# The small stack fourth instead of first, and a ring of expert slabs that starts with six buffers

## The chip, the cores and the metric

The kernel runs on one core of a Trainium2 chip. The metric is the device time of one execution in microseconds (us). Before the change the median of three runs is 1639.17 us (1639.06 to 1639.73).

## What is computed

One decoder layer for 256 tokens of width 2048, all in 32-bit floats. The first part mixes tokens by two paths (latent attention and a gated linear recurrence). The change touches the second part only, the mixture of experts:

```python
g_sel = jnp.argmax(g_logits, axis=-1)                   # one of 4 groups of experts
top_p, top_i = lax.top_k(jax.nn.softmax(e_in, axis=-1), TOP_K)   # two of its 8 experts
weights = g_w[:, None] * top_p / jnp.sum(top_p, axis=-1, keepdims=True)
...
hg = jnp.einsum('td,edf->tef', t, w_gate_e[sl])         # 2048 x 512 for each expert
hu = jnp.einsum('td,edf->tef', t, w_up_e[sl])
act = jax.nn.silu(hg) * hu * comb[:, sl, None]
out = out + jnp.einsum('tef,efd->td', act, w_down_e[sl])   # 512 x 2048
```

Of 32 experts each token uses two, so most experts see few tokens, but the weights of nearly all of them must be read: 12 MiB for each.

## The kernel before

The mixer and the router take the first 780 us or so. The router counts the tokens of each expert and sorts the experts by that count: rank 0 is the expert with the most tokens. Expert number 0 and the expert of rank 0 are computed *dense*, for all 256 tokens; ranks 1 and 2 form a *stack* in which each expert has 64 columns of TensorE for its tokens, and ranks 3 to 26 form six stacks of four experts with 32 columns each. A last stack (ranks 27 to 30) and a loop for experts with too many tokens run only if there is something to do.

Each expert's weights lie in DRAM as 12 slabs of 1 MiB, 8 for gate and up and 4 for down. A stack goes through them in 12 *groups*: a group takes the same slab of each of its experts, so two or four slabs, and multiplies them side by side on TensorE (line 1285). Group 0 to 7 are gate and up (`gu`), then follows the activation (`s`, the transposes `ab`, the copy `aT`), and groups 8 to 11 are down (`yb`), each followed by multiplies that put the tokens back (`ob`). Before a stack begins, its tokens are gathered (`prep`, the tiles `cb`, `xb`, `xg`). A group is 8 multiplies of 64 columns with two experts, and 16 of 32 columns with four.

The slabs of the stacks land in a *ring* of buffers (`fetch_used`). As long as the list `room` has an entry, a load takes a new buffer; then each load takes the oldest buffer of the ring and has to wait until TensorE is through with the group that reads it. Loads are issued by SyncE's queue in the order in which the code calls for them, and one that waits holds up all behind it. I number them: load 1 is the first into the ring, and there are 312.

Dense experts use other buffers. Their slabs (`raw` for the first six, then `rawb`, two buffers) are split by ScalarE and VectorE into a high and a low half (`whl`, lines 186 and 187), and 48 multiplies (lines 199 to 201) use each slab. The ring's buffers come from the pool `big` of nine, in which `raw` lives too, so a ring buffer can have to wait for a dense slab to be split.

The main loop interleaves two streams: `heavy` (the dense experts) and `light` (the stacks), by the share of each that is done. A light step is one group and counts its slabs, 2 or 4; a dense step counts 0.5. After a stack's activation one dense step is put in between. When the dense stream has ended, which it does after 120 loads, five more buffers join the ring, one with each group (`later`). The order on SyncE is the order of the code; on the other engines a scheduler places the instructions at build time.

Of the kernel before, what the change touches and what calls it, by code (L numbers as in the profile page):

```python
# [29 lines left out]
B2 = 10  # L30
SKIP = [0, 1]
BIG2 = 4
RING = 7
EARLY = (1, 1)
AHEAD2 = 6
AHEAD_B = 2
# [29 lines left out]

DENSE = 0
HEAVY = [("dense", 0)]
LIGHT = [("stack", 1, 2)] + [("stack", r, 4) for r in (3, 7, 11, 15, 19, 23)]
LAST = ("stack", 27, 4)  # L70


# [1 line left out]
def decoder_layer_kernel(ctx, tc, xT, c, pos, cols_d, const_d, mask_d, w_ada, w_head, w_half, w_blk, w_mlv, w_pa, w_pb, w_out,  # L74
# [988 lines left out]

    ring = []

    room = [u8] * RING

    def fetch_used(src, rank):
        if room:
# [145 lines left out]
    def expert(r):  # L1215
        if r not in reg:
            reg[r] = nc.sync.value_load(R["order"][0:1, r:r + 1], min_val=0, max_val=NE - 1)
        return reg[r]
# [143 lines left out]
    def unit(u):  # L1362
        if u[0] == "dense":
            r = u[1]
            return dense(lambda: expert(r), lambda: R["perm"][:, r:r + 1].to_broadcast([32, P]), lambda: R["qT"][:, 1], xgh, xgl)
        return stack(u[1], u[2], u is LIGHT[-1])

    def stream(units, gen=None):
        ready = lambda u: u[0] == "dense" or u[1] in pre
        for i in range(-1 if gen else 0, len(units)):  # L1370
            if i >= 0:
                if not ready(units[i]):
                    pre[units[i][1]] = prep(*units[i][1:])
                gen = unit(units[i])
            for what in gen:
                if what != "act":
                    yield what
                else:
                    if i + 1 < len(units) and not ready(units[i + 1]):
                        pre[units[i + 1][1]] = prep(*units[i + 1][1:])  # L1380
                    yield "act"

    heavy, light = stream(HEAVY, first), stream(LIGHT)
    n_light = 12.0 * sum(u[2] for u in LIGHT)
    n_heavy = HEAVY_SHARE * n_light
    streams, total, done = [heavy, light], (n_heavy, n_light), [started, 0.0]
    forced, later = [], [v8] * 2 + [w8] * W4
    while any(streams):
        i = forced.pop(0) if forced else int(done[0] / total[0] > done[1] / total[1])
        if not streams[i]:  # L1390
            i = 1 - i
        got = next(streams[i], None)
        if got == "act":
            forced = [1 - i] * SKIP[i]
        elif got:
            done[i] += got
            if not streams[0] and later:
                room.append(later.pop(0))
        else:
            streams[i] = None  # L1400
# [158 lines left out]
```

## Time and profile before

| what | value |
|---|---|
| median of three runs | 1639.17 us |
| profiled execution | 1639.2 us, of which the traced span is 1637.3 us |
| TensorE (PE) busy | 1378.5 us, 84% of the span |
| VectorE (DVE) busy | 815.3 us, 50% |
| ScalarE (ACT) busy | 504.2 us, 31% |
| moved by DMA | 560.96 MB, mean 343 GB/s |
| chain that ended last | 33% of it in loads into the ring |

The busy shares are means over two unlike halves. Up to about 780 us TensorE is busy nearly without a break; in the stacks it is not, and the transfers are. Which of the two a stretch waits for is read from the views by stretch.

### The profile page before, as it was taken

What the parts mean: (1) busy time and instruction counts of PE and PEld (TensorE: products, weight loads), DVE (VectorE), ACT (ScalarE), POOL (GpSimd) and SP (SyncE); (2) the same over time, 40 slices, a digit from 0 to 9 for tenths busy, and PEclk for the clock granted to TensorE, in tenths of its full rate; (3) what the DMA queues carried; (4) which work ended last, traced back from release to release, by engine and by line L of the source; (5) the groups of instructions that cost most, each with busy time, mean ns of one, the idle gap of its engine ahead of it and who ended that gap; (6) DMA issues with size and microseconds to landing.
All of it is one profiled execution on the core that took longest, in us unless ns stands there. A gap on an engine that the chain in (4) does not pass through costs nothing.

```text
span 1637.3 us, 24656 instructions
## 1 busy us (share of the span) xinstructions
PE 1378.5 (84%) x9726; PEld 1009.6 (62%) x9726; DVE 815.3 (50%) x1177; ACT 504.2 (31%) x720; POOL 87.4 (5%) x91
## 2 busy tenths in 40 slices
PE   7899998999999999999989689868767656657675
PEld 5698997999999989999747356535413213213212
DVE  5878699879776789986414233224301201201102
ACT  3134765446755574445312121212001001001000
POOL 0150014000000010121000000000000000000000
PEclk9899999999999999999999889998868878888888
DMA  9978767878676779874597999999999999999995
GB/s 383 374 283 329 282 212 283 327 286 296 245 273 242 269 267 416 321 297 155 224 409 273 416 400 378 420 417 393 399 421 422 420 422 421 420 422 421 421 421 228
DMA packets 78462, 560.96 MB, mean 343 GB/s; under 512 B 8705, under 2 KB 8961, under 8 KB 11905
## 3 DMA queue, kind: packets, MB, share of 16 engines
q1 hardware_dynamic: 78050, 558.84, 86.5%
q8 instruction: 80, 1.31, 0.3%
q10 hardware_dynamic: 288, 0.45, 0.1%
q14 instruction: 44, 0.36, 0.1%
HBM read 569.74 MB, written 2.10 MB: 349 GB/s over the span
## 4 chain that ended last, share of the span: by engine, by line
PE 50%; DMA 33%; DVE 6%; ACT 3%; issue 2%; POOL 1%; SPq 0%; DVEq 0%; POOLq 0%; ACTq 0%
DMA ring<-in_w_gu_dram 22%; DMA ring<-in_w_dn_dram 11%; PE gu L1285 6%; PE ga L199 4%; PE yb L1285 4%; PE ga L201 3%; PE ga L200 3%; DVE whl L187 2%; PE hp L201 2%; PE hp L199 2%; PE hp L200 2%; PE xb L1259 2%; PE wo L199 1%; DVE raw L143 1%; PE wo L201 1%
## 5 line engine op out<-in xcount | busy, mean ns | idle before, releaser
L1285 PE MATMUL gu<-ring,xg 128*32 128x512 f32 (+1 forms) x1664 | 270.4, 756 | 138.0 <-DMA ring<-in_w_gu_dram 138.0
L187 DVE TENSOR_TENSOR whl<-raw,whl 128x1024 fp32r<-128x1024 f32 (+1 forms) x222 | 267.1, 1210 | 93.1 <-ACT whl L186 92.6
L186 ACT ACTIVATE whl<-raw 128x1024 fp32r<-128x1024 f32 (+1 forms) x222 | 229.5, 1038 | 255.3 <-PE ga L201 62.7
L1285 PEld LDWEIGHTS gu<-ring,xg 128*32 128x32 f32 (+1 forms) x1664 | 65.7, 136 | 324.6 <-DMA ring<-in_w_gu_dram 172.0
L143 DVE SCALAR_TENSOR_TENSOR raw<-raw,cond 128x2048 f32<-128x2048 f32 x96 | 220.3, 2296 | 16.5 <-DMA raw<-in_w_ada_dram 16.4
L1285 PE MATMUL yb<-ring,aT 128*32 128x512 f32 (+1 forms) x832 | 130.7, 725 | 64.0 <-DMA ring<-in_w_dn_dram 61.9
L199 PE MATMUL ga<-hh,whl 128*128 128x256 f32 x512 | 149.6, 292 | 0.0
L201 PE MATMUL ga<-hh,whl 128*128 128x256 f32 x512 | 145.0, 283 | 1.4 <-DVE whl L187 1.3
L200 PE MATMUL ga<-hl,whl 128*128 128x256 f32 x512 | 144.8, 283 | 0.0
L1285 PEld LDWEIGHTS yb<-ring,aT 128*32 128x32 f32 (+1 forms) x832 | 33.5, 131 | 145.2 <-issue 99.6
L1231 DVE SCALAR_TENSOR_TENSOR xs<-ob,mod,xs 128x256 f32<-128x256 f32 x112 | 46.5, 477 | 131.9 <-PE ob L1325 131.9
L1251 DVE TENSOR_REDUCE wc<-cb 128x1 f32<-128x256 f32 x7 | 3.0, 424 | 215.8 <-PE cb L1248 215.8
L199 PEld LDWEIGHTS ga<-hh,whl 128*128 128x128 f32 x512 | 97.9, 191 | 5.1 <-issue 3.5
L201 PEld LDWEIGHTS ga<-hh,whl 128*128 128x128 f32 x512 | 97.9, 191 | 2.0 <-DVE whl L187 2.0
L200 PEld LDWEIGHTS ga<-hl,whl 128*128 128x128 f32 x512 | 98.0, 191 | 1.0 <-issue 0.7
L187 DVE TENSOR_TENSOR whl<-rawb,whl 128x1024 fp32r<-128x1024 f32 x36 | 43.0, 1221 | 110.7 <-ACT whl L186 110.7
L1303 ACT ACTIVATE s<-gu 128x512 f32<-128x512 f32 x7 | 4.2, 594 | 295.8 <-PE gu L1285 295.8
L201 PE MATMUL hp<-hh,whl 128*128 128x256 f32 x320 | 91.7, 287 | 3.4 <-DVE whl L187 3.3
L199 PE MATMUL hp<-hh,whl 128*128 128x256 f32 x320 | 92.6, 290 | 0.0
L200 PE MATMUL hp<-hl,whl 128*128 128x256 f32 x320 | 91.2, 285 | 0.0
L1314 ACT ACTIVATE yh<-yb 128x512 fp32r<-128x512 f32 x28 | 16.8, 599 | 190.2 <-PE yb L1285 190.2
L186 ACT ACTIVATE whl<-rawb 128x1024 fp32r<-128x1024 f32 x36 | 36.7, 1050 | 122.6 <-DMA rawb<-in_w_gu_dram 59.7
(418 smaller groups left out, 2905.6 us busy)
## 6 DMA issues: line engine op xcount, KB each, us to landing
ring<-in_w_gu_dram SPq DMA_DIRECT2D x208, 1024.0 KB, 14.8
ring<-in_w_dn_dram SPq DMA_DIRECT2D x104, 1024.0 KB, 15.1
raw<-in_w_ada_dram SPq DMA_DIRECT2D x96, 1024.0 KB, 6.8
raw<-in_w_blk_dram SPq DMA_DIRECT2D x32, 1024.0 KB, 5.1
raw<-in_w_half_dram SPq DMA_DIRECT2D x20, 1024.0 KB, 6.9
raw<-in_w_out_dram SPq DMA_DIRECT2D x16, 1024.0 KB, 6.5
raw<-in_w_head_dram SPq DMA_DIRECT2D x16, 704.0 KB, 7.8
rawb<-in_w_gu_dram SPq DMA_DIRECT2D x10, 1024.0 KB, 10.4
```

Source lines behind the costliest of these rows:

```text
L143: vec.scalar_tensor_tensor(raw, raw, 1.0, cond, op0=ALU.mult, op1=ALU.mult, accum_out=mod[:, i:i + 1])
L186: keep(act.activation(hi, raw, AF.Copy))
L187: keep(vec.tensor_tensor(lo, raw, hi.bitcast(F32), op=ALU.subtract))
L199: pe.matmul(out, wh, xh, start=first, stop=False)
L200: pe.matmul(out, wh, xl, start=False, stop=False)
L201: pe.matmul(out, wl, xh, start=False, stop=last)
L1231: vec.scalar_tensor_tensor(xs[:, d], src, mod[:, 80 + d:81 + d], xs[:, d], op0=ALU.mult, op1=ALU.add)
L1251: vec.tensor_reduce(wc, cb[:, :T], axis=AX.X, op=ALU.add)
L1259: pe.matmul(b[:, i * P:(i + 1) * P], xr[tt][:, k * P:(k + 1) * P], gt[tt], start=tt == 0, stop=tt == 1)
L1285: return lambda: pe.matmul(out[j * C:(j + 1) * C, :], x[:, k * P + j * C:k * P + (j + 1) * C], ws[j][:, cut], start=first, stop=stop)
L1303: act.activation(s, gu[0], AF.Silu)
L1314: act.activation(yh, yb, AF.Copy)
```

## The change

The list of stacks has the stack of ranks 1 and 2 in fourth place instead of first; ranks 3, 7 and 11 come ahead of it. The ring starts with six buffers instead of seven, and a seventh is added to `room` once 12 slabs are done, so that load 13, the first of the fourth group, takes it. The five later buffers join as before.

```diff
-RING = 7
+FIRST_RING = 6
...
-LIGHT = [("stack", 1, 2)] + [("stack", r, 4) for r in (3, 7, 11, 15, 19, 23)]
+LIGHT = [("stack", r, 4) for r in (3, 7, 11)] + [("stack", 1, 2)] + [("stack", r, 4) for r in (15, 19, 23)]
...
-    room = [u8] * RING
+    room = [u8] * FIRST_RING
...
             done[i] += got
+            if i == 1 and done[1] == 4 * FIRST_RING / 2:
+                room.append(u8)
             if not streams[0] and later:
                 room.append(later.pop(0))
```

On SyncE's queue, loads 6 to 8 of the ring stood like this before. The names `DVE`, `PE`, `Activation` and `DMAHW` in brackets are the semaphores that an instruction waits for: the engine that has to be through, or an earlier transfer. A `TENSOR_LOAD` reads whether an expert has tokens.

```order
L1071 DMA ring<-in_w_gu_dram 128x2048 [waits DMAHW6_49,DVE_49]
L1071 ISA
L1071 DMA ring<-in_w_gu_dram 128x2048 [waits DMAHW7_49,DVE_49]
L1224 TENSOR_LOAD order
L1224 ISA x2
L1074 ISA
L1074 REGISTER_ALU
L1074 ISA
L1074 DMA ring<-in_w_gu_dram 128x2048 [waits DMAHW1_49,DMAHW0_49,PE_49]
```

And now, loads 6 and 7:

```order
L1071 DMA ring<-in_w_gu_dram 128x2048 [waits DMAHW6_49,DVE_49]
L1224 TENSOR_LOAD order
L1224 ISA x2
L1074 ISA
L1074 REGISTER_ALU
L1074 ISA
L1074 DMA ring<-in_w_gu_dram 128x2048 [waits DMAHW7_49,DMAHW1_49,PE_49]
```

The seventh load waited for a dense slab (VectorE); it now waits for TensorE to be through with the first group. The new seventh buffer stands six loads further on, as load 13, ahead of load 14:

```order
L1074 DMA ring<-in_w_gu_dram 128x2048 [waits DMAHW6_49,PE_49]
L1071 ISA
L1071 DMA ring<-in_w_gu_dram 128x2048 [waits DVE_49]
L1074 ISA
L1074 REGISTER_ALU
L1074 ISA
L1074 DMA ring<-in_w_gu_dram 128x2048 [waits DMAHW7_49,PE_49]
```

On TensorE the first stack's last gate and up groups, the gather for the second stack (`cb`, `xb`) and the first down groups stood like this before, where `64x512 x40` are five groups of two slabs:

```order
L201 MATMUL gu<-xgh,whl 128x258
L1285 MATMUL gu<-ring,xg 64x512 x40
L1248 MATMUL cb<-const,G 128x128 x2
L1259 MATMUL xb<-G,xr 128x128 x8
L1285 MATMUL gu<-ring,xg 64x512 x8
L1259 MATMUL xb<-G,xr 128x128 x24
L1308 MATMUL ab<-const,s 128x128 x4
L1285 MATMUL yb<-ring,aT 64x512 x16
```

And now, where `32x512 x48` are three groups of four slabs:

```order
L201 MATMUL gu<-xgh,whl 128x258
L1285 MATMUL gu<-ring,xg 32x512 x48
L1248 MATMUL cb<-const,G 128x128 x2
L1259 MATMUL xb<-G,xr 128x128 x24
L1285 MATMUL gu<-ring,xg 32x512 x16
L1259 MATMUL xb<-G,xr 128x128 x8
L1308 MATMUL ab<-const,s 128x128 x4
L1285 MATMUL yb<-ring,aT 32x512 x32
```

Between these groups stand the first dense expert's multiplies, 261 of its gate and up part from the first gather on. Before, in the order of the program: 31, group 0 of the stack of two, 23, group 1, 15, groups 2 to 6, the last gate and up group, three down groups with 25 dense multiplies between, 23, then 63, group 0 of the stack at rank 3, 74, its group 1, and the last 7. Now: 69, groups 0 and 1 of the stack at rank 3, 68, group 2, 74, group 3, 50, and groups 4 to 6 behind one another.

## Rows read from the trace of the kernel before

**Rows 1.** The page's section 2: 40 equal slices of the span

```profile
DMA  9978767878676779874597999999999999999995
GB/s 383 374 283 329 282 212 283 327 286 296 245 273 242 269 267 416 321 297 155 224 409 273 416 400 378 420 417 393 399 421 422 420 422 421 420 422 421 421 421 228
```

**Rows 2.** Busy time by stretch: length, engines (instructions), TensorE clock, DMA share, GB/s

```profile
800.00:811.00 11.00, 11.00 (x68) 6.45 (x68) 2.45 (x2) 2.12 (x2) 0.00 (x0) 1.00 0.03 7
811.00:850.00 39.00, 34.27 (x187) 16.81 (x183) 6.71 (x17) 7.38 (x16) 0.00 (x0) 0.96 1.01 412
850.00:875.00 25.00, 25.00 (x151) 14.88 (x152) 11.43 (x25) 6.38 (x11) 0.00 (x0) 1.00 0.97 361
875.00:900.00 25.00, 24.88 (x206) 18.80 (x204) 7.45 (x11) 3.95 (x8) 0.00 (x0) 1.00 0.55 218
900.00:960.00 60.00, 40.43 (x304) 22.25 (x304) 17.83 (x34) 8.18 (x10) 0.00 (x0) 0.87 1.01 413
960.00:1000.00 40.00, 36.40 (x289) 25.64 (x289) 15.51 (x27) 11.35 (x17) 0.00 (x0) 0.89 0.91 361
1100.00:1150.00 50.00, 40.85 (x317) 27.58 (x318) 24.00 (x49) 12.84 (x20) 0.00 (x0) 0.90 0.94 381
```

**Rows 3.** What SyncE's transfer queue waited for, 780 to 900: total, times, longest

```profile
SPq L1074 <- PE gu L1285: 33.7, 6, 14.6
SPq L1071 <- DVE whl L187: 22.8, 2, 16.0
SPq L1074 <- PE yb L1285: 15.4, 3, 8.9
```

**Rows 4.** Timeline of SyncE: issues into the ring (start, us to the last's end)

```profile
809.62 0.33 SPq L1071 DMA_DIRECT2D ring<-in_w_gu_dram  x1
885.58 2.62 SPq L1074 DMA_DIRECT2D ring<-in_w_gu_dram  x4
```

**Rows 5.** The ring's instructions, 780 to 830: from issue to landing

```profile
DMA to landing us min/median/max: 4.7/10.5/13.8
```

**Rows 6.** Timeline of TensorE: first dense multiply, first group, the group of load 8

```profile
797.75 0.36 PE L199 MATMUL gu<-xgh,whl 128*128 128x258 f32 x1
801.64 0.65 PE L1285 MATMUL gu<-ring,xg 128*64 128x512 f32 x2
817.91 3.65 PE L1285 MATMUL gu<-ring,xg 128*64 128x512 f32 x16 [0.50 <-DMA ring<-in_w_gu_dram]
```

**Rows 7.** The chain that ended last: start, us, what (x counts trace records)

```profile
791.08 6.92 PE xb L1259 x62
801.71 3.58 PE gu L1285 x16
881.99 3.57 PE gu L1285 x32
908.46 6.07 DMA ring<-in_w_gu_dram
914.57 5.19 PE gu L1285 x32
919.76 7.19 DMA ring<-in_w_gu_dram
927.00 3.66 PE gu L1285 x32
```

**Rows 8.** Busy time by stretch, as in rows 2: one wait, and the later stacks

```profile
1140.00:1145.00 5.00, 3.86 (x20) 0.99 (x24) 0.00 (x0) 0.00 (x0) 0.00 (x0) 0.50 1.01 424
1200.00:1600.00 400.00, 259.24 (x1674) 88.61 (x1666) 44.87 (x106) 22.61 (x44) 0.00 (x0) 0.82 1.01 421
```

## The prediction

> **What bounds the kernel now.** I read four views in this order. First the page's row of bytes per second: from about the 23rd of its 40 slices on it stands near 420 GB/s until the last slice [rows 1]. The second half of the program is a stream of expert weights, and its length is the bytes left divided by that rate, plus every microsecond in which the transfers did not run at it. So I looked for those microseconds, with the busy times by stretch [rows 2]. 1 MiB at 421 GB/s takes 2.49 us. Measured against 421, the stretches lose (length times one minus rate over 421): 800 to 811, 10.8 us; 811 to 850, 0.8; 850 to 875, 3.6; 875 to 900, 12.1; 900 to 960, 1.1; 960 to 1000, 5.7; 1100 to 1150, 4.8; after 1200 nothing. About 39 us in all, and each one that goes away ends the program one microsecond sooner, as long as nothing later runs dry instead.
>
> Who made the queue wait there is told by the waits of the transfer queue between 780 and 900 [rows 3]: for a ring buffer that TensorE still reads (33.7 and 15.4 us), and for the seventh buffer, which held a dense slab until VectorE had split it (22.8 us). The issue times show both: the seventh load goes out at 809.62 although the first six had landed by 800, and nothing goes out until 885.58 after the loads had run out at about 877 [rows 4]. Between 875 and 900 TensorE is busy 24.88 of 25 us [rows 2]: this is the passage from the stack of two to the first stack of four. There the scheduler put 63 and then 74 dense multiplies around the first group of four, while the ring held seven loads, one group and three quarters. No buffer came free, so no load could go out.
>
> **The change, step by step.** The bytes stay the same: the same 26 ranks, the same 12 slabs each, the same dense slabs at the same numbers of loads. So the sum is made of idle stretches of the transfer queue alone. The bricks, each from a row: a load lands at the earliest 4.7 us after its issue [rows 5], which is 2.2 us and then 2.49 us of bytes; loads behind it follow every 2.49 us. TensorE starts a group 1.1 us after its last load landed (load 7 goes out at 809.62, so load 8 lands at 816.8, and the group starts at 817.91 [rows 4, 6]). A group takes 3.6 us, of two slabs or of four alike, and 5.3 us when TensorE had waited some microseconds before it [rows 7]. A dense multiply takes 0.12 us: 31 of them fill 797.75 to 801.64 [rows 6]. A gather multiply takes 0.22 us: 62 records, two to a multiply, fill 6.92 us [rows 7].
>
> I call groups 0 to 7 the gate and up groups of the stack at rank 3, which now comes first. Before group 0 stand 69 dense multiplies instead of 31: 797.75 + 69 x 0.12 = 806.0, and group 0 ends at 809.6. Loads 7 to 10 take its buffers and run from 811.8. Before, load 7 also ran from 811.8, so the first gap stays as it is: the seventh buffer no longer blocks the queue, but group 0 is later by as much. This edit I cost at nothing.
>
> Then come new gaps, since a group now takes four of six buffers. Group 1 needs load 8 (816.8), starts at 817.9 after 8.3 us of waiting, ends at 823.2. Loads 7 to 10 ran out at 821.8, and loads 11 to 15 run from 825.4: a gap of 3.6. (Load 13 is the seventh buffer; its dense slab is split by then, as the dense multiplies that use it stand before group 0. Were it not, loads 14 and 15 would wait behind it.) 68 dense multiplies last until 831.4; group 2 runs 831.5 to 835.1, in time: no gap. 74 more, and group 3 runs 844.0 to 847.6, while the queue is full only until 847.8: gap 2.0. 50 more; group 4 runs 853.6 to 857.2, no gap. Group 5 starts when load 24 has landed, 863.4, ends at 868.7: gap 1.2. Group 6 likewise, 874.5 to 879.8: gap 1.1. 26 gather multiplies and transposes, then group 7, 885.6 to 889.2: no gap. Group 8, the first down group, 895.6 to 900.9: gap 1.1. Together 9.0 us, and load 40 has landed at 811.8 + 34 x 2.49 + 9.0 = 905.5.
>
> Before, load 40 stood behind the losses of 811 to 900, 0.8 + 3.6 + 12.1, and about 0.8 of those up to 912: 17.3 us. The stream is then ahead by 17.3 - 9.0 = 8.3 us. The 12.1 us go because the passage from a stack of two to a stack of four no longer happens beside the dense expert: the order has the first dense expert's 261 remaining gate and up multiplies done before group 4, where before the last of them stood behind the second group of four. The 3.6 us of 850 to 875 are a lower rate at a busy share of 0.97 [rows 2], while few loads were under way; I let them go too, since groups of four put four loads in the queue at a time, and from 900 to 960, where they did so, the rate was 413 [rows 2].
>
> After load 40 the dense slabs stand at the same loads in the queue, and the ring grows by five at the same load, so the rest moves as a block. Two things in it are unlike. The passages inside and between stacks beside the dense experts cost 5.7 us at 960 to 1000 and 4.8 at 1100 to 1150 [rows 2]. After the change, the passage inside the stack at rank 7 is in the order what the costly one of before was (24 dense, 32 gather, 24 dense multiplies on end between groups), and the passage inside the stack at rank 3 now stands before the dense down work and is in the gap of 1.1 already. What remains is whether the second is gone or moves to the stack at rank 11: between 0 and 4.8 us of gain. I take 0, the rate rows of the stack having no other cause that goes. The stack of two itself now runs on twelve buffers: 5.0 us of loads to a group of 3.6 us. Its group can be later than the loads by ten buffers, 24.9 us, before the queue notices; I cost it at nothing.
>
> TensorE's waits have a price of their own. A group after 6.07 us of waiting took 5.19 us, one after 7.19 us, with dense work in the middle of it, 3.66 [rows 7]; that is in the sum as 5.3 for groups 1, 5, 6 and 8. The Trainium skill has a rule for this (TensorE: Matmul & The Clock Gate, section "Loop structure matters more than you think"): a wait for a transfer in the middle of a loop lets the clock fall to half. It speaks against a ring of six, which adds such waits, and the trace agrees. Without its effect, with 3.6 us for every group, the gaps would shrink to about 3.9 us and the sum would be -13.4, some 1626.
>
> The sum is made against the profiled execution, 1639.2 us for a span of 1637.3; the median of the runs is 1639.17, the same within 0.1. 1639.2 - 8.3 = 1630.9, say 1631.
>
> **The rivals.** *The starved ring* (slower). While only a few loads are under way, the rate may be the 361 GB/s of 850 to 875 [rows 2] instead of 421. If all of loads 7 to 40 run so, 34 x 2.49 x (421/361 - 1) = 14.1 us come on top: -8.3 + 14.1 = +5.8, 1645. It decides from a mean rate, while busy, of about 380 on. Against it: at 811 to 850 as few loads were under way, and the rate was 412 [rows 2].
> *The late stack of two* (slower). Where TensorE idles, the granted clock is 0.50, and 0.82 on average after 1200 [rows 8]. At half clock a group takes 7.2 us and needs loads of 5.0; eight groups fall 17.6 us behind, the gather of the next stack takes 13.8, four down groups 8.8 more: 40 us against a cover of 24.9. The queue stops for 15, and the end is 1639.2 - 8.3 + 15 = 1646. It decides when the lag passes 24.9 us. Against it: the same groups ran at 0.96 and 1.00 from 811 to 875 [rows 2], where TensorE had work without end.
> *The round trip is longer than I count.* If the answer from a group's end to a landed load is 1.3 us longer in each of the five gaps, 6.5 of the 8.3 us are eaten: 1637, no change that can be told. For it: the middle time to landing is 10.5 us [rows 5], though mostly by queueing.
> *More is gained.* The passage at 1100 to 1150 goes too: 1639.2 - 8.3 - 4.8 = 1626.
>
> **Chances.** Forecast 0.54, more gained 0.20, longer round trip 0.13, starved ring 0.09, late stack of two 0.04. A measurement can tell about 0.2%, 3.3 us, from no change. Faster: the forecast (but for 0.02 at its upper edge) and the larger gain, 0.72; same: the round trip and that edge, 0.15; slower: 0.13. The range reaches from the larger gain with 2 us to spare, 1624, to just past the round trip's case, 1640; beyond it lie the two slower rivals.
>
> **What will show it.** Right: between 800 and 811 the queue idle as before; four short gaps and no long one up to 905; TensorE waiting some 8 us before the second group of the stream, then 5 to 6 us before groups 5 and 6; no stretch without a load at 877 to 887; the ring's fifth load of growth about 8 us earlier than before; 421 GB/s on twelve buffers throughout the stack of two. Wrong: a rate below 400 with a busy share near 1 before 905 (starved ring), a queue that waits for a TensorE group of the stack of two (late stack), or the lead of 8 us that is there at load 40 and gone at load 125.

## The result, and the profile after

Eight runs of the changed kernel have a median of 1631.42 us, eight of the kernel before 1640.26; the ratio is 0.9947, with a 95% interval of 0.993 to 0.9963. That is 8.7 us less by the ratio (6 to 11.5 by its interval), where 8.3 were forecast. The size of the whole was right, in part by luck: the lead that was forecast for load 40 came out too large, and what was forecast to stay the same behind it did not.

Busy time by stretch in the kernel after; the columns are those of [rows 2], the last one is GB/s:

```profile
811.00:850.00 39.00, 34.51 (x275) 24.90 (x276) 7.33 (x11) 5.30 (x5) 0.00 (x0) 0.89 0.88 354
850.00:875.00 25.00, 13.87 (x92) 4.51 (x94) 0.00 (x0) 0.69 (x4) 0.00 (x0) 0.77 0.93 380
875.00:900.00 25.00, 20.27 (x158) 10.81 (x150) 4.79 (x11) 4.74 (x10) 0.00 (x0) 0.88 0.97 398
900.00:960.00 60.00, 44.39 (x312) 28.24 (x309) 26.62 (x51) 10.28 (x13) 0.00 (x0) 0.83 0.94 368
960.00:1000.00 40.00, 33.08 (x260) 21.31 (x264) 9.66 (x12) 6.01 (x6) 0.00 (x0) 0.96 1.01 421
1100.00:1150.00 50.00, 37.17 (x274) 23.07 (x270) 16.47 (x28) 7.59 (x9) 0.00 (x0) 0.90 0.96 392
1200.00:1600.00 400.00, 272.54 (x1707) 98.30 (x1711) 55.17 (x132) 25.01 (x48) 0.00 (x0) 0.86 1.01 421
```

The long hole is gone: 218 GB/s from 875 to 900 in [rows 2], now 398. In its place the queue is a little short of bytes from 811 to 875, and again from 900 to 960. Loss against 421 GB/s in us, worked out as in the prediction (length times one minus rate over 421) from one row for each stretch, for the two traces of before and three of after:

| stretch | before | before again | after | after again | after, third |
|---|---|---|---|---|---|
| 797 to 811 | 11.5 | 11.7 | 11.4 | 11.9 | 11.6 |
| 811 to 850 | 0.8 | 0.7 | 6.2 | 6.6 | 6.3 |
| 850 to 900 | 15.6 | 15.4 | 3.8 | 3.8 | 3.8 |
| 900 to 960 | 1.1 | 1.3 | 7.6 | 4.7 | 4.6 |
| 960 to 1000 | 5.7 | 5.8 | 0.0 | 0.0 | 0.0 |
| 1000 to 1100 | 0.5 | 2.1 | 4.5 | 3.3 | 3.6 |
| 1100 to 1200 | 5.0 | 5.7 | 3.6 | 2.9 | 3.8 |
| sum in us | 40.2 | 42.7 | 37.1 | 33.2 | 33.7 |

The chain that ended last shows what the gaps are made of (start, us, what). It goes from the first group to the down groups of the first stack:

```profile
803.18 3.70 PE gu L1285 x32
808.13 7.22 DMA ring<-in_w_gu_dram
815.49 5.54 PE gu L1285 x32
829.38 3.57 PE gu L1285 x32
842.01 3.57 PE gu L1285 x32
851.80 3.59 PE gu L1285 x32
855.39 6.25 DMA ring<-in_w_gu_dram
861.67 6.36 PE gu L1285 x32
868.03 4.76 DMA ring<-in_w_gu_dram
872.83 5.87 PE gu L1285 x32
...
884.44 3.59 PE gu L1285 x32
888.02 6.99 DMA ring<-in_w_dn_dram
895.15 4.98 PE yb L1285 x32
900.13 7.03 DMA ring<-in_w_dn_dram
907.30 5.71 PE yb L1285 x32
```

Each long group stands behind a wait for a load, each short one behind dense or gather work, as [rows 7] had it. Read these times from the first load into the ring, not from the start: that load was issued at 779.66 here and at 782.77 in the first trace of before, and in the repeats at 782.05, 781.08 and 781.70, so a lead of 3 us is not in every trace of the change, and it arises ahead of the first load into the ring.

### The profile page after: what moved, and what is told of

It reads as the page before. It is cut to its first block, busy times and chain, and to the rows that moved or that the text cites. A ratio compares the mean times of both kernels' runs of the same rounds, so it can differ in the third digit from the quotient of the medians.

```text
span 1632.3 us, 24652 instructions
## 1 busy us (share of the span) xinstructions
PE 1360.1 (83%) x9726; PEld 1004.2 (62%) x9726; DVE 816.4 (50%) x1177; ACT 504.9 (31%) x720; POOL 90.5 (6%) x91
## 4 chain that ended last, share of the span: by engine, by line
PE 51%; DMA 34%; DVE 9%; ACT 3%; issue 2%; POOL 0%; SPq 0%; DVEq 0%; POOLq 0%; ACTq 0%
DMA ring<-in_w_gu_dram 22%; DMA ring<-in_w_dn_dram 11%; PE gu L1285 6%; PE ga L199 4%; PE ga L201 4%; PE ga L200 4%; DVE raw L143 4%; PE yb L1285 3%; DVE whl L187 2%; PE hp L201 2%; PE hp L199 2%; PE hp L200 2%; PE xb L1259 2%; PE wo L199 1%; PE wo L201 1%
## 5 line engine op out<-in xcount | busy, mean ns | idle before, releaser
L1285 PE MATMUL gu<-ring,xg 128*32 128x512 f32 (+1 forms) x1664 | 256.5, 714 | 131.2 <-DMA ring<-in_w_gu_dram 131.0
L1285 PEld LDWEIGHTS yb<-ring,aT 128*32 128x32 f32 (+1 forms) x832 | 33.7, 131 | 156.9 <-issue 115.9
L201 PE MATMUL gu<-xgh,whl 128*128 128x258 f32 x256 | 72.1, 285 | 2.2 <-DVE whl L187 2.2
```

The lines of the kernel that those rows point to most:

```text
L201: pe.matmul(out, wl, xh, start=False, stop=last)
L1285: return lambda: pe.matmul(out[j * C:(j + 1) * C, :], x[:, k * P + j * C:k * P + (j + 1) * C], ws[j][:, cut], start=first, stop=stop)
```

## The experiments

**Which half of the change does it.** The new list with the old ring, and the new ring with the old list.

```diff
-LIGHT = [("stack", 1, 2)] + [("stack", r, 4) for r in (3, 7, 11, 15, 19, 23)]
+LIGHT = [("stack", r, 4) for r in (3, 7, 11)] + [("stack", 1, 2)] + [("stack", r, 4) for r in (15, 19, 23)]
```

> The new list of stacks, with the old ring of seven from the start. Theory A (the gain is the passage from a stack of two to a stack of four that no longer stands beside the dense expert): all of the gain stays, and as much as 3 us more, since load 7 then needs only a split dense slab and may go out before the first group ends: 1626 to 1632 where the kernel before takes 1640, ratio 0.991 to 0.996. Theory B (the gain is the seventh buffer that no longer blocks the queue): no gain is left, 1638 to 1642, ratio 0.999 to 1.001.

Measured: 1625.95 us, ratio 0.9926 (0.9904 to 0.9947). The other half alone, the six buffers and the seventh from 12 slabs on:

> The old list of stacks, with the ring of six and the seventh buffer joining once 12 slabs are done. Theory A: the 10 us without a transfer at the passage from two to four stay; only load 7 goes out some 4 us sooner, at the end of the first group of two: 1636 to 1640, ratio 0.997 to 1.000. Theory B: the gain of the change is here, 1630 to 1633, ratio 0.993 to 0.996.

Measured: 1635.84 us, ratio 0.9977 (0.9963 to 0.999). Both as theory A had them by the ratio; both medians lie at the lower edge of its range, 0.05 and 0.2 us below. The list alone takes 14 us by the medians and 12 by the ratio, more than the whole change; the ring alone takes 4 with the old list. These 4 us rest on the twelve runs: the kept trace of the second kernel is of its slowest run, 1645.0 us. The hole at the passage is still there in the second kernel, by its stretch:

```profile
875.00:900.00 25.00, 24.09 (x199) 18.02 (x197) 7.37 (x11) 4.25 (x8) 0.00 (x0) 1.00 0.53 214
```

The two halves don't add up: 12 and 4 apart, 9 together, all by the ratios. With the old list the ring of six frees the queue of a load that waits for a dense slab: load 7 goes out 22.6 us after the first load, where it was 26.9. With the new list that slab is split sooner, since 69 dense multiplies stand ahead of the first group; load 7 goes out before the first group, not after it. Issue of load 7, in the new list with the old ring, and in the second trace of the changed kernel:

```profile
804.72 0.33 SPq L1071 DMA_DIRECT2D ring<-in_w_gu_dram  x1
```

```profile
809.16 0.33 SPq L1074 DMA_DIRECT2D ring<-in_w_gu_dram  x1
```

Counted from the first load (781.62 and 782.05) that is 23.1 against 27.1 us. The two kernels had not run side by side so far; now they did:

> The new list with the old ring of seven once more, beside the changed kernel on the same chip. Theory A (the ring of six costs what load 7 waits longer, the end of the first group instead of a split slab, some 3 us): 1624 to 1629, 2 to 6 us below the changed kernel. Rival I (the two rings are alike, and the difference between the two kernels was chance): within 1.5 us of it.

> The changed kernel once more, for the pair with the old ring in the new list: 1628 to 1634 by theory A, and by rival I the same time as that kernel.

Measured: 1627.79 us (0.9926, 0.9903 to 0.9949) for the old ring in the new list, 1631.48 us (0.9945, 0.9926 to 0.9964) for the changed kernel. The difference is 3.7 us by the medians and 3.1 by the ratios; in the first comparison it was 5.5 and 3.4. The intervals of the two ratios overlap, but of the 48 pairs that the six and the eight runs make here, the old ring is the faster in 46. The traces have the place: from 797 to 900 the old ring in the new list loses 19.2 and 19.4 us, the changed kernel 21.4, 22.3 and 21.7. Rival I is not supported.

**How much of a trace is chance.**

> The kernel before, unchanged, for a second trace. If the lead in the traces is real, the first load into the ring goes out at about the same time in every trace (779 to 784), and the time from it to the group that takes load 121 is 391 to 395 us, as in the first trace (393).

> The changed kernel, unchanged, for a second trace. In the first, the first load went out at 779.7, 3 us sooner than before, and the group with load 121 started 391.1 us after it. Theory A: 384 to 392 us again, the start of the first load is chance. Rival C (part of the gain lies ahead of the stacks, by another placement of instructions): the first load is again 3 us earlier than in the kernel before.

Measured: first load at 781.70 and 782.05, so rival C falls as it was stated, with 3 us in every trace. A smaller lead is not excluded: the four traces with the stack of two first, of all runs in this document, have the first load at 781.7 to 784.8 (mean 783.3), the nine with another list at 779.7 to 782.9 (mean 781.5), and no run shows what sets it. From there to the group that takes load 121 it was 396.3 us in the kernel before (393.1 in the first trace) and 386.5 in the changed one (391.1 in the first, 386.6 in the third). The expectation of 391 to 395 for before was missed by 1.3 us: two traces of one kernel differ by 3 to 5 us in this stretch. The means, 394.7 and 388.1, are 6.6 us apart; the times, from more runs, 8.7. One pair of traces, the first, shows 2.0 us, and would have made the mechanism look too small.

**Is it the passage between the two kinds of stack?** The stack of two in second place, and in last:

> Ring of seven, the stack of two second: behind the stack at rank 3, ahead of that at rank 7. Theory A (a stack of two beside the dense experts costs by its passages and by its groups, which take TensorE 3.6 us for 5.0 us of loads with dense work between): some 6 to 10 us more than with the stack of two fourth, 1632 to 1636, with a stretch without loads of some 7 us at its passage. Rival D (only the very first stack matters, since it fills the ring): no loss against the stack of two fourth, 1624 to 1628.

> Ring of seven, the stack of two last, behind rank 23 to 26. Theory A: behind the dense experts its place is without effect on the stream, 421 GB/s throughout; the end differs by what stands behind the last load (a group of two and its tokens): 1624 to 1628, ratio 0.990 to 0.995. Rival (the late stack of two is bound by TensorE): the queue waits for its groups, some 10 us more, 1634 to 1638.

Measured: 1639.63 us (0.999, 0.9976 to 1.0005) in second place, and 1627.05 (0.9921, 0.9902 to 0.994) in last. Last is as good as fourth: once the dense experts are done, the place is without effect, and the rival of a late stack bound by TensorE falls. Second is as bad as first, worse than theory A had it. With the stack of two second, two stretches stand out:

```profile
1000.00:1050.00 50.00, 49.38 (x348) 32.80 (x347) 18.06 (x31) 11.64 (x21) 0.00 (x0) 1.00 0.85 341
1100.00:1150.00 50.00, 40.86 (x308) 28.12 (x300) 23.06 (x47) 12.76 (x20) 0.00 (x0) 0.86 0.89 362
```

In the first TensorE is busy 49.38 of 50 us while the queue loses 9.5, as in [rows 2] at 875 to 900. The second loses 7.0, and is the passage inside the stack at rank 7, with the same series of dense and gather multiplies as before the change. Moving the small stack also moves what falls beside such a passage. Theory A had priced only the first.

To see the passage apart from the list, the old list and ring with fewer dense multiplies in that place:

```diff
-HEAVY_SHARE = 0.2
+HEAVY_SHARE = 0.15
```

> The old list and the old ring, the stack of two first; only the share by which the dense stream is mixed in is 0.15 instead of 0.2, so that no dense multiplies stand between the stack of two and the first group of the stack of four, and 25 fewer inside the stack of two. Theory A (the idle 10 us at the passage from two to four are dense multiplies that stand there while the ring is full): from 850 to 900 the queue loses 3 to 6 us against 421 GB/s instead of 15.6, with the stack of two still first. The time gains less, since the dense stream ends later and the ring grows later: 1632 to 1638. Rival H (a stack of two first costs by itself, by the ring of seven holding three groups of two but not two of four): the 12 us at 875 to 900 stay, 1638 to 1642.

Measured: 1640.95 us, ratio 1.0004 (0.9987 to 1.0022). Its stretches:

```profile
850.00:875.00 25.00, 22.70 (x117) 9.38 (x120) 11.26 (x26) 5.23 (x11) 0.00 (x0) 0.93 0.99 397
875.00:900.00 25.00, 25.00 (x212) 18.07 (x205) 6.13 (x5) 5.30 (x5) 0.00 (x0) 1.00 0.92 369
900.00:960.00 60.00, 39.92 (x268) 18.51 (x267) 13.08 (x27) 7.05 (x12) 0.00 (x0) 0.80 0.94 378
```

From 850 to 900 it loses 4.5 us instead of 15.6, with the stack of two still first. So the hole is the dense work at the passage, as theory A said, and rival H falls. The time, though, lies above the range: the gain is given back, 6.1 us at 900 to 960 where the kernel before lost 1.1, 5.5 at 1000 to 1100 where it lost 0.5, and 5.5 at 1200 to 1300 where it lost none. The last dense multiply ends at 1258 us instead of 1165, and the ring stays small that much longer.

**The loss that I had not foreseen, at 900 to 960.** In the changed kernel the chain there runs through the dense expert's own activation:

```profile
PEld dd L199 <- ACT ath L943: 5.1, 1, 5.1
PE dd L199 <- ACT ath L943: 4.7, 1, 4.7
```

These are its waits from 900 to 960 (total, times, longest). The dense down multiplies (`dd`) wait for the activation (`ath`), and the third down group of the stack is queued behind them on TensorE. TensorE's timeline has it in order, and SyncE's has the issue of load 44, the last of that group:

```profile
919.44 0.80 PE L199 MATMUL dd<-ath,whl 128*128 128x256 f32 x2 [4.67 <-ACT ath L943]
...
925.17 1.06 PE L1285 MATMUL yb<-ring,aT 128*32 128x512 f32 x8
```

```profile
913.03 0.33 SPq L1074 DMA_DIRECT2D ring<-in_w_dn_dram  x1
```

In the run below, where this group does not stand behind the activation, it began 5.6 us after the issue of its last load (910.13 to 915.70). By that, an estimate, it could begin here at 918.6; it begins at 925.17, and its four buffers come free some 6.6 us later. To test it, on the new list with the old ring, one group of the stack was put between:

```diff
-SKIP = [0, 1]
+SKIP = [1, 1]
```

> Order of the change, ring of seven, and one light step forced behind a dense expert's activation, so that a group of the stack stands between the dense expert's gate and down work. Theory E (the 5 us lost at 905 to 935 in the changed kernel are TensorE waiting for the dense activation on VectorE and ScalarE, with a group queued behind that wait): the wait moves beside a group, 3 to 5 us less than without it, 1621 to 1624. Rival F (that loss is the dense slabs in the queue, not the activation): no change, 1625 to 1628.

Measured: 1627.15 us, ratio 0.9926 (0.9905 to 0.9946); without the edit 1625.95 and 1627.79. The wait is gone from the trace, and the loss at 900 to 960 fell, here first without and then with the edit:

```profile
900.00:960.00 60.00, 44.98 (x338) 28.92 (x338) 26.67 (x51) 10.64 (x14) 0.00 (x0) 0.89 0.96 391
1000.00:1150.00 150.00, 118.80 (x941) 79.84 (x940) 49.13 (x85) 29.85 (x47) 0.00 (x0) 0.92 0.99 408
```

```profile
900.00:960.00 60.00, 45.95 (x355) 28.85 (x356) 29.36 (x54) 11.43 (x15) 0.00 (x0) 0.91 1.00 409
1000.00:1150.00 150.00, 117.47 (x925) 76.74 (x924) 49.37 (x86) 29.97 (x47) 0.00 (x0) 0.91 0.98 401
```

4.3 us became 1.7 (3.6 in the second trace without the edit, 2.6 in the next run, which has it too), but from 1000 to 1150 4.6 became 7.1. That the wait causes much of this loss is shown; that it costs time is not. Theory E is right on the wait and wrong on the end. Why the later stretch loses more is open: two traces of one kernel differ by as much, and in the next run it loses 4.3.

> As the kernel with the light step behind the dense activation, and without the dense step that is forced behind a stack's own activation, so that the passage from gate and up to down has 24 dense multiplies fewer. Theory A: the 5 us without loads in the passage of the stack at rank 7 shrink by about 3, and the one of the stack at rank 11 likewise by up to 1: 1617 to 1621. Rival G (TensorE has nothing else to do while the activation runs, so that the step only moves): as without it, 1621 to 1624.

This was `SKIP = [1, 0]`. Measured: 1626.62 us, ratio 0.993 (0.9906 to 0.9953), against 1627.15 without this second edit: no gain that can be told from the spread of the runs, and both times that were named were too low, by 2.6 us and more. In the traces theory A has the passage of the stack at rank 7 right. Its stretches, first without and then with the edit:

```profile
1045.00:1050.00 5.00, 5.00 (x44) 2.19 (x43) 0.32 (x1) 0.80 (x2) 0.00 (x0) 1.00 0.54 200
1050.00:1055.00 5.00, 5.00 (x47) 4.27 (x49) 0.37 (x1) 0.00 (x0) 0.00 (x0) 1.00 0.90 367
```

```profile
1045.00:1050.00 5.00, 5.00 (x45) 3.11 (x38) 3.05 (x3) 1.64 (x3) 0.00 (x0) 1.00 0.92 359
1050.00:1055.00 5.00, 5.00 (x44) 5.00 (x43) 0.00 (x0) 0.00 (x0) 0.00 (x0) 1.00 0.99 403
```

They lose 3.3 us without and 0.9 with. The 24 multiplies that are taken out stand behind the first down group instead, where 42 dense multiplies have become 66. From 797 to 1200 the two traces lose 28.4 and 26.4 us, and the profiled executions are 1.1 us apart, so a small gain is neither shown nor excluded.

The best version is the new list with the ring of seven from the start, 1626 to 1628 us in two comparisons. None of the further edits improved on it clear of the spread.

## Why the prediction was right, and where it was not

*The stream of loads is the bound, and what counts are the stretches in which it does not run at 421 GB/s.* Right, and the runs leave little beside it. From 1200 on the rate is 420 or 421 in every kernel but the one with the dense share of 0.15, and the losses ahead of it order the kernels: 40 and 43 us before, 33 to 37 after, 29 with the new list and the old ring. Take from each of the 13 profiled executions the time of its first load and its losses from 797 to 1300; what remains is 814.9 to 817.5 us. So these two numbers account for the differences of up to 21 us between them to within 2.6.

*The first gap stays.* Right for this kernel: load 7 went out 26.9 us after the first load before, and 27.1, 27.1 after. But the reason was half of the truth. I compared the ring of six with the old kernel, not with a ring of seven in the new list. The edit costs nothing against what was there, and 3 to 4 us against what could have been. The 0 in my sum holds against the kernel before; it says nothing of the choice between the two rings.

*Five small gaps of 9.0 us up to load 40.* Mostly right. TensorE waited 8.74 us for the second group (8.86 and 9.03 in the other traces), 8.3 forecast:

```profile
815.49 5.54 PE L1285 MATMUL gu<-ring,xg 128*32 128x512 f32 x32 [8.74 <-DMA ring<-in_w_gu_dram]
```

The first three gaps are in the 5 us stretches of the kernel after:

```profile
810.00:815.00 5.00, 0.00 (x0) 0.00 (x0) 0.00 (x0) 0.00 (x0) 0.00 (x0) 0.50 0.98 377
815.00:820.00 5.00, 4.51 (x27) 1.28 (x30) 0.00 (x0) 0.00 (x0) 0.00 (x0) 0.56 0.81 339
820.00:825.00 5.00, 5.00 (x45) 4.16 (x38) 0.00 (x0) 0.86 (x1) 0.00 (x0) 1.00 0.57 197
845.00:850.00 5.00, 5.00 (x45) 4.49 (x38) 0.00 (x0) 0.00 (x0) 0.00 (x0) 1.00 0.69 251
865.00:870.00 5.00, 3.00 (x20) 0.59 (x12) 0.00 (x0) 0.00 (x0) 0.00 (x0) 0.79 0.66 239
```

The first gap lies across 820: 1.0 us of it before and 2.7 behind, 3.6 in all, as I had it. The next two lose 2.0 and 2.2 us, where I had 2.0 and 1.2; the group behind the third took 6.4 us instead of the 5.3 of my sum. From 811 to 900 the three traces lose 10.0, 10.4 and 10.1, and 1.6 more by 905 in the first: 11.6 against 9.0. The rest of the difference is in lesser dips between the gaps.

*The lead at load 40 is 8.3 us.* Too large. The group with load 40 began 131.8 and 132.0 us after the first load before, and 127.6, 127.2 and 126.6 after: a lead of 4.8. The 17.3 us that I took away went (the kernel before lost 16.5 from 811 to 905), but more came in their place than the 9.0. At load 121 the lead is 6.6, and the times are 8.7 apart. In the traces, 8.3 us apart in the mean, 6.8 are fewer losses and 1.3 an earlier first load, which my sum does not have. So that the whole came out within 0.4 us of the forecast is partly luck.

*After that the rest moves as a block.* This is the step that failed, though the range held. The costly passage inside a stack of four did move as forecast to the second of them, from 960 to 1000 (5.7 us) to 1050 to 1060, where it costs 3.2 to 4.2. But the dense expert's activation came to stand between the down groups and had a group wait behind it: 900 to 960 lost 4.6 to 7.6 us instead of 1.1 (1.6 of the 7.6 before 905), and the passage at 1100 to 1150, which I had left at nothing, lost 1.4 to 3.4 instead of 4.8. I had followed TensorE's and SyncE's order and the ring, not the waits of the dense multiplies for VectorE and ScalarE; the order showed them, with the first dense down multiplies close behind `cw`.

*The rivals.* The starved ring: the rate in stretches with few gaps was 398 to 421 in the rows above, so it did not decide. The late stack of two: 421 GB/s from 1200 to 1300, where TensorE was busy 80 of 100 us at a granted clock of 0.96; before, it was busy 66 at 0.79. The longer round trip: the first answer took 0.4 to 0.7 us longer than counted, not 1.3, and the gaps together 2.6 us more, not 6.5. More gained: it was to be had, but by the other ring.

## What to carry to other kernels

Before you price a new buffer or one less, ask what holds the buffer in the *new* order, not in the old one: the same edit gained 4 us with one list and lost 3 to 4 with the other. Where two streams share an in-order engine, look for the place where a group of one stands behind a long run of the other while the ring is full; by the counts here the ring sets how long such a run may be, though no run beside the dense expert had a ring longer than seven. And a wait removed in the middle of a stream that is bound elsewhere is not yet time: three of the edits here (the dense share at 0.15, the light step moved, the step left out) took a wait or a hole out of its place and left the time of the kernel they were made in, as far as the spread of the runs lets one tell.

## What the runs showed of the hardware

A group of two experts with 64 columns each and one of four with 32 columns each took TensorE the same 3.6 us, so a slab of the small stack costs twice the time of another. After waits of 4.7 to 8.7 us a group of the first stack took 5.0 to 6.4 us, with a granted clock of 0.50 and 0.56 in the rows of 810 to 820 above, about half of full speed, 1.2 instead of 2.4 GHz. And single traces of one kernel were up to 5 us apart at load 121. The stretches in which they part can be named (900 to 960, 7.6 against 4.7 us), but no run shows why: a mechanism of 5 us needs more than one pair.
